# Layer 1 of a hybrid encoder: x brought into token form by VectorE block transposes and a trip through DRAM instead of TensorE transposes

## The chip, the cores and the metric

One Trainium2 chip, one of its cores. The metric is the device time of one execution in microseconds (us); lower is better. The kernel before was run three times: 1388.98, 1391.51 and 1394.25 us, median 1391.51 us. One more execution was profiled; it took 1389.59 us, and its span in the trace is 1387.7 us.

The engines are called by the names of the profile: PE (TensorE, matrix multiplication), PEld (its weight loads), DVE (VectorE), ACT (ScalarE), POOL (GpSimd) and SP (SyncE, which here only issues DMAs). Each engine works through its own list of instructions strictly in order; an instruction that waits holds up all that is behind it on its engine.

## What is computed

Two layers over 272 tokens (16 meta tokens and 256 frames) of width 2048, fp32 throughout. Layer 0 mixes gated linear attention and stick-breaking attention. Layer 1, the one that is changed, is a Mamba-2 mixer with 8 groups of 8 heads (head dimension 64, state 128). Cut to what matters here:

```python
z, xbc, dt_raw = split(h @ w_in)                 # 4096, 4096 + 2*1024, 64 columns
xbc = silu(causal_depthwise_conv(xbc))           # 4 taps
xs, bs, cs = split(xbc)                          # x: 8 groups x 8 heads x 64
dt  = softplus(dt_raw + dt_bias)
xdt = xs * dt[..., None]
a_cum = cumsum(dt * -exp(a_log))                 # per head
y = sum over s <= t of exp(a_cum[t] - a_cum[s]) * (c[t] . b[s]) * xdt[s]  + d_skip * xs
y = rms_norm_groups(y * silu(z), norm_w)
f = y @ w_out
h = layer_norm(ALPHA * h + f)
```

The kernel does not chunk: for one group it forms the matrix M (tokens s by tokens t, one for each head) = exp(decay difference) times (b . c), and y = xdt^T M. For that product xdt must lie with tokens on the partitions, while the projection, the convolution and the SiLU leave x with channels on the partitions. Bringing x from channel form into token form is what the change is about.

## The kernel before

**Weights and projections.** All large matmuls are done in three fp32r passes (high by high, high by low, low by high; helper `three`, lines L178 to L180, and L494 to L496 for the output projection). Weights come in units of 128 x 2048 fp32 (1 MB), loaded by SP on one queue (`load_unit`, L144) into three buffers `raw`, then cut in halves of 128 x 1024 into a high part `whi` (ACT, L159) and a low part `wlo` (DVE, a few on POOL, L160). There are five buffers for `whi` and `wlo` each. A unit that projects in (`in1`) is 48 matmuls of 256 to 272 columns, one that projects out (`out1`) 24 of 512 columns.

**Order of layer 1.** For each group g the units are B, C, x0, x1, x2, x3, z0, z1, z2, z3 (group 0: z0 before x0); from group 2 on, each group's ten units are followed by the four units of out1(g-2). While PE runs these units, side tasks advance by one step at each `tick` (four ticks in a unit); a bare `yield` in a task costs one tick. The instructions that come out of this are then ordered by a scheduler in the framework, engine by engine; a few runs of PE instructions are pinned together.

**The decays.** `dt_path` computes dt and the cumulated decays with heads on partitions, writes them to DRAM (`edr`), and takes their token form by small TensorE transposes into `est` and `est2` (the last 16 tokens). For each group `load_decay` (called by `post_B`, for group 0 by `decay1`) reads them back, broadcast over the partitions, into `ebc` (128 x 3328 fp32, 1664 KB, L1072). `ebc` lies in the buffer tagged `hacc`, of which there is one. `decay1` waits for the mixer of the group before, then makes M from `ebc` and `est` (L1105, L1106 on DVE, exp on ACT at L1108, the 16-token corner `mt` at L1112), and multiplies it by b . c (L1133). There is one buffer for M.

**The path of x.** Units x0 to x3 give four tiles of 128 channels x 272 tokens in `xt`. `post_x` does the convolution (L1050), and for each pair starts `x_path(g, j)`: SiLU (L1057, three ACT passes, the product at L1061), and for the second pair, after waiting steps, 8 TensorE transposes of 128 x 128 (L1173) and 4 of 128 x 16 (L1177) against the identity, into PSUM. DVE then multiplies by dt out of PSUM, into `xd` (four instructions, L1186) and `xd2` (four, the last 16 tokens, L1192).

**The mixer.** `mix_ssd` waits for the decay, x and z, then PE forms y = xdt^T M (L1235 with `xd` and M, L1241 with `xd2` and `mt2`), pinned in one block; DVE, POOL and ACT finish y (L1245 to L1255), PE sums the squares (L1261).

Of the kernel before, what the change touches and what calls it, by code (L numbers as in the profile page):

```python
# [6 lines left out]
F32 = mybir.dt.float32  # L7
F32R = mybir.dt.float32r
AF = mybir.ActivationFunctionType
ALU = mybir.AluOpType  # L10
PSUM = bass.MemoryType.PSUM

P = 128
D = 2048
KT = 16
NM = 16
S = 256
C0 = 12
NFIRST = 6
T = NM + S  # L20
# [10 lines left out]
NG, HPG = 8, 8  # L31
# [51 lines left out]
def _wait(*tasks):  # L83
    for t in tasks:
        while not t.done:
            yield


class _Body:
# [904 lines left out]
    def dt_path(self, ps, scr):  # L994
# [3 lines left out]
        H = 64  # L998
# [32 lines left out]
        self.est2 = lp.tile([16, 2, H], F32, tag="est2", name="est2")  # L1031
# [7 lines left out]
        vec.tensor_copy(self.est2.rearrange("p a h -> p (a h)"), pt[:16, 256:384])  # L1039
# [29 lines left out]
    def load_decay(self, g):  # L1069
        eb = self.hp.tile([P, HPG, 416], F32, tag="hacc", name=self.nm("ebc"))  # L1070
        src = self.edr[g * HPG : (g + 1) * HPG, :].rearrange("h c -> (h c)").partition_broadcast(P)
        self.nc.sync.dma_start(eb.rearrange("p h c -> p (h c)"), src)  # L1072
        self.cur["ebc", g] = eb
# [5 lines left out]
    def decay1(self, g):  # L1079
# [5 lines left out]
        if g:  # L1085
            yield from _wait(*self.mixers[6 + g - 1])
        else:
            yield from _wait(self.tasks["dt"], self.tasks["res"])
            self.load_decay(0)
            yield  # L1090
            yield
# [19 lines left out]
        e2 = self.est2[:, 0, g * HPG : (g + 1) * HPG].rearrange("p (h o) -> p h o", o=1).broadcast_to([16, HPG, 16])  # L1111
# [40 lines left out]
    def x_path(self, g, j):  # L1152
        nc, vec = self.nc, self.nc.vector
        xt = self.cur["x", g]
        xd = self.cur["xd", g]
        self.silu1(xt[:, j : j + 2, :].rearrange("p a t -> p (a t)"), vec)
        yield
        yield
        yield
        if g == 0:  # L1160
            yield from _wait(self.tasks["dt"])
        if j == 0:
            return
        for _ in range(5):
            yield
        pin = self.tc.keep_in_program_order

        pts = [self.po(), self.po()]
        p2 = self.zbank()
        for pt, jj in zip(pts, (0, 2)):  # L1170
            for i in range(2):
                for t in range(2):
                    pin(nc.tensor.transpose(  # L1173
                        pt[:, t * 256 + i * P : t * 256 + (i + 1) * P], xt[:, jj + i, t * P : (t + 1) * P], self.ident
                    ))
        for i in range(4):
            pin(nc.tensor.transpose(p2[:16, i * P : (i + 1) * P], xt[:, i, 256:T], self.ident))  # L1177
        yield
        hv = lambda a: a.rearrange("p (h c) -> p h c", c=64)
        bd = lambda a: a.rearrange("p (h o) -> p h o", o=1)  # L1180
        for pt, jj in zip(pts, (0, 2)):
            h0 = g * HPG + 2 * jj
            c = slice(jj * P, jj * P + 256)
            for t in range(2):
                d = bd(self.est[:, 1, t, h0 : h0 + 4]).broadcast_to([P, 4, 64])
                vec.tensor_tensor(hv(xd[:, t, c]), hv(pt[:, t * 256 : (t + 1) * 256]), d, op=ALU.mult)  # L1186
            yield
        e2 = bd(self.est2[:, 1, g * HPG : (g + 1) * HPG])
        for j in range(2):
            for p in range(2):  # L1190
                h = 4 * p + 2 * j
                vec.tensor_tensor(  # L1192
                    self.xd2[32 * j : 32 * j + 16, 2 * p : 2 * p + 2, :], hv(p2[:16, :])[:, h : h + 2, :],
                    e2[:, h : h + 2, :].broadcast_to([16, 2, 64]), op=ALU.mult,
                )
        yield
# [262 lines left out]
```

## Time and profile before

| what | value |
|---|---|
| runs, median (lowest to highest) | 1391.51 us (1388.98 to 1394.25) |
| profiled execution, its own time | 1389.59 us |
| span of the profiled execution | 1387.7 us |
| PE busy / DVE busy / ACT busy / POOL busy | 99% / 73% / 56% / 19% of the span |
| granted clock of PE | 1.00 of full speed |
| DMA | 249.83 MB, queue q1 takes 51.0% of the 16 DMA engines' span |
| layer 1 in the trace | from about 737 us to the end |

In the rows below, "busy" is time in which an engine executes; matmuls overlap, so the duration of one (0.28 us) is longer than the distance between the starts of two. "idle before <- releaser" is time in which the engine stood, and whose work ended it. Where a row counts a line's instructions, "x64" is how many there are.

### The profile page before, as it was taken

The numbers are of one execution on the slowest core, as the hardware profiler recorded it, in microseconds if no ns is written. First come the engines' busy times: TensorE is split into PE (matmuls) and PEld (weight loads), VectorE is DVE, ScalarE is ACT, GpSimd is POOL, SyncE is SP. The second block draws the span as 40 slices with busy tenths as digits, with TensorE's granted clock in tenths as the row PEclk, the third lists the DMA queues.
The fourth block names the chain that finished last, engine by engine and source line by source line (L and its number), as shares of the span: only waits on it lengthen the run. The fifth ranks groups of instructions, "written<-read, shape, count | busy, mean of one in ns | idle before, by whom it ended". The sixth has DMA issues, their size and how long they took to land.

```text
span 1387.7 us, 26097 instructions
## 1 busy us (share of the span) xinstructions
PE 1379.2 (99%) x10715; PEld 1328.3 (96%) x10715; DVE 1017.3 (73%) x1690; ACT 771.7 (56%) x1149; POOL 260.6 (19%) x253
## 2 busy tenths in 40 slices
PE   9999999999999999999999999999999999999998
PEld 8999999999999999999999999899898999989986
DVE  7857575574565565557899999787877778867687
ACT  6645454454345544556587677565565655656551
POOL 0000010100101000113500153331322323133221
PEclk9999999999999999999999999999999999999999
DMA  8544544445454445544354655465555556455561
GB/s 320 185 161 156 181 154 171 163 156 179 156 179 156 153 152 179 174 151 148 122 199 169 251 202 201 158 256 174 213 180 187 197 187 228 164 200 185 179 216 61
DMA packets 38007, 249.83 MB, mean 180 GB/s; under 512 B 4288, under 2 KB 6144, under 8 KB 9472
## 3 DMA queue, kind: packets, MB, share of 16 engines
q1 hardware_dynamic: 37168, 247.38, 51.0%
q8 instruction: 84, 1.38, 0.4%
q10 hardware_dynamic: 720, 0.79, 0.2%
q14 instruction: 35, 0.29, 0.1%
HBM read 245.94 MB, written 2.20 MB: 179 GB/s over the span
## 4 chain that ended last, share of the span: by engine, by line
PE 94%; DVE 3%; DMA 1%; ACT 1%; POOL 1%; issue 0%; SPq 0%; ACTq 0%; POOLq 0%; DVEq 0%
PE pj L179 25%; PE pj L178 25%; PE pj L180 25%; PE pj L494 4%; PE pj L496 4%; PE pj L495 4%; PE po L1235 1%; PE po L608 1%; DVE wlo L160 1%; PE po L1173 0%; DMA raw<-in_wts 0%; PE po L587 0%; PE z L1123 0%; POOL yu L1246 0%; DVE M L1105 0%
## 5 line engine op out<-in xcount | busy, mean ns | idle before, releaser
L178 PE MATMUL pj<-xhi,whi 128*128 128x272 f32 (+4 forms) x2560 | 732.1, 286 | 1.3 <-DVE fix L936 0.5
L179 PE MATMUL pj<-xlo,whi 128*128 128x272 f32 (+4 forms) x2560 | 730.8, 286 | 0.0
L180 PE MATMUL pj<-xhi,wlo 128*128 128x272 f32 (+4 forms) x2560 | 730.1, 286 | 0.0
L159 ACT ACTIVATE whi<-raw 128x1024 fp32r<-128x1024 f32 (+2 forms) x434 | 449.6, 1039 | 423.8 <-PE pj L179 350.7
L160 DVE TENSOR_TENSOR wlo<-raw,whi 128x1024 fp32r<-128x1024 f32 (+2 forms) x405 | 503.3, 1247 | 242.0 <-ACT whi L159 237.4
L178 PEld LDWEIGHTS pj<-xhi,whi 128*128 128x128 f32 x2560 | 482.1, 189 | 3.7 <-ACT whi L159 0.9
L179 PEld LDWEIGHTS pj<-xlo,whi 128*128 128x128 f32 x2560 | 482.1, 188 | 1.5 <-DVE wlo L160 0.4
L180 PEld LDWEIGHTS pj<-xhi,wlo 128*128 128x128 f32 x2560 | 481.9, 188 | 1.0 <-issue 0.8
L178 PE MATMUL pj<-mixh,whi 128*128 128x272 f32 x384 | 110.5, 289 | 0.0
L180 PE MATMUL pj<-mixh,wlo 128*128 128x272 f32 x384 | 110.5, 288 | 0.0
L179 PE MATMUL pj<-mixl,whi 128*128 128x272 f32 x384 | 110.4, 288 | 0.0
L160 POOL TENSOR_TENSOR wlo<-raw,whi 128x1024 fp32r<-128x1024 f32 x29 | 73.0, 2517 | 192.6 <-ACT whi L159 192.6
L494 PE MATMUL pj<-whi,yh 128*128 128x512 f32 (+1 forms) x240 | 93.3, 389 | 0.0
L495 PE MATMUL pj<-wlo,yh 128*128 128x512 f32 (+1 forms) x240 | 92.6, 386 | 0.0
L496 PE MATMUL pj<-whi,yl 128*128 128x512 f32 (+1 forms) x240 | 92.2, 386 | 0.0
L261 POOL TENSOR_TENSOR gr<-gr,gsc 128x1088 f32<-128x1088 f32 x6 | 15.4, 2568 | 308.2 <-ACT gsc L260 308.2
L179 PEld LDWEIGHTS pj<-mixl,whi 128*128 128x128 f32 x384 | 72.3, 188 | 0.2
L180 PEld LDWEIGHTS pj<-mixh,wlo 128*128 128x128 f32 x384 | 72.3, 188 | 0.1
L178 PEld LDWEIGHTS pj<-mixh,whi 128*128 128x128 f32 x384 | 72.2, 188 | 0.1
L503 DVE SCALAR_TENSOR_TENSOR acc<-pj,rr,acc 128x512 f32<-128x512 f32 (+1 forms) x65 | 46.5, 734 | 13.9 <-PE pj L496 13.9
L496 PEld LDWEIGHTS pj<-whi,yl 128*128 128x128 f32 x240 | 45.1, 188 | 9.1
L494 PEld LDWEIGHTS pj<-whi,yh 128*128 128x128 f32 x240 | 45.1, 188 | 9.0
(351 smaller groups left out, 1472.2 us busy)
## 6 DMA issues: line engine op xcount, KB each, us to landing
raw<-in_wts SPq DMA_DIRECT2D x212, 1024.0 KB, 4.8
ebc<-edr SPq DMA_DIRECT2D x8, 1664.0 KB, 6.7
raw<-in_wts SPq DMA_DIRECT2D x9, 256.0 KB, 6.4
hacc<-in_xT SPq DMA_DIRECT2D x7, 272.0 KB, 5.3
early<-in_wts SPq DMA_DIRECT2D x2, 512.0 KB, 6.5
lg<-in_lnr SPq DMA_DIRECT2D x1, 1024.0 KB, 4.7
lb<-in_lnr SPq DMA_DIRECT2D x1, 1024.0 KB, 5.3
out_h<-acc SPq DMA_DIRECT2D x2, 384.0 KB, 2.4
```

Of the source, the lines that this page charges most:

```text
L159: self.nc.scalar.activation(hi, src, AF.Copy)
L160: eng.tensor_tensor(lo, src, hi.bitcast(F32), op=ALU.subtract)
L178: mm(ps, whi, xhi, start=first, stop=False)
L179: mm(ps, whi, xlo, start=False, stop=False)
L180: mm(ps, wlo, xhi, start=False, stop=last)
L261: mul(c, c, e, op=ALU.mult)
L494: mm(ps, yh[:, kk, tt], hi[:, k, :], start=kk == 0, stop=False)
L495: mm(ps, yh[:, kk, tt], lo[:, k, :], start=False, stop=False)
L496: mm(ps, yl[:, kk, tt], hi[:, k, :], start=False, stop=kk == 3)
L503: self.nc.vector.scalar_tensor_tensor(a, ps, r[:, t : t + 1], a, op0=ALU.mult, op1=ALU.add)
L608: mm = lambda r, a, b, start=False, stop=False: self.nc.tensor.matmul(o[:, r], a, b, start=start, stop=stop, skip_group_check=True)
L1235: pin(mm(ov[p][i * 64 : (i + 1) * 64, jj, t0:S], xd[:, s, h * 64 : (h + 1) * 64], M[:, h, c0:c1], start=(s, jj) == (0, 0), stop=False, **gk,))
```

## The change

`x_path` no longer uses TensorE. Of the `hacc` buffer, whose 4352 columns `ebc` fills to 3328, the remaining 1024 columns become `xs`. After the SiLU of each pair DVE transposes the pair's 256 frame columns in blocks of 32 x 32 into `xs`, and the last 32 token columns into a new small tile `x9`. For the second pair SP then writes `xs` (512 KB) and `x9` (64 KB) to DRAM tiles `xdr` and `xdr9`; three ticks later it reads them back so that tokens come to lie on partitions: four DMAs of 128 KB into the place of `xs` (runs of 128 elements) and two of 16 KB into `xd2` (runs of 32). Three ticks later DVE multiplies by dt, now from SBUF: four instructions into `xd`, two in place in `xd2`. `est2` is kept on 48 partitions, with a second copy, for this. Since `xs` and `ebc` share one buffer, the next group's `load_decay` can only be issued when the products of this group have read `xs`. In `decay1`, groups after the first take three more ticks after the wait for the mixer before. The waits of `x_path` go from 3 and 5 ticks to 1, 3 and 3.

```diff
--- before.py
+++ after.py
@@ -1028,7 +1028,7 @@
         nc.sync.dma_start(self.edr, E[:, 16:432])
         yield
         self.est = lp.tile([P, 2, 2, H], F32, tag="est", name="est")
-        self.est2 = lp.tile([16, 2, H], F32, tag="est2", name="est2")
+        self.est2 = lp.tile([48, 2, H], F32, tag="est2", name="est2")
         yield from _wait(self.tasks["res"])
         pt = self.po()
         for n, a in enumerate((E[:, 0:128], E[:, 272:400], m[:, 0:128], m[:, 128:256])):
@@ -1036,7 +1036,8 @@
         for n, a in enumerate((E[:, 416:432], m[:, 256:272])):
             nc.tensor.transpose(pt[:16, 256 + n * H : 256 + (n + 1) * H], a, self.ident[:H, :H])
         vec.tensor_copy(self.est.rearrange("p a b h -> p (a b h)"), pt[:, :256])
-        vec.tensor_copy(self.est2.rearrange("p a h -> p (a h)"), pt[:16, 256:384])
+        for q in (0, 32):
+            vec.tensor_copy(self.est2[q : q + 16].rearrange("p a h -> p (a h)"), pt[:16, 256:384])
         yield
 
     def conv(self, src, ct, v, t0=0, lo=0):
@@ -1067,7 +1068,9 @@
             self.load_decay(g)
 
     def load_decay(self, g):
-        eb = self.hp.tile([P, HPG, 416], F32, tag="hacc", name=self.nm("ebc"))
+        eb = self.hp.tile([P, KT * T], F32, tag="hacc", name=self.nm("ebc"))
+        self.cur["xs", g] = eb[:, HPG * 416 :].rearrange("p (b c x) -> p b c x", c=4, x=32)
+        eb = eb[:, : HPG * 416].rearrange("p (h c) -> p h c", h=HPG)
         src = self.edr[g * HPG : (g + 1) * HPG, :].rearrange("h c -> (h c)").partition_broadcast(P)
         self.nc.sync.dma_start(eb.rearrange("p h c -> p (h c)"), src)
         self.cur["ebc", g] = eb
@@ -1084,6 +1087,9 @@
         yield
         if g:
             yield from _wait(*self.mixers[6 + g - 1])
+            yield
+            yield
+            yield
         else:
             yield from _wait(self.tasks["dt"], self.tasks["res"])
             self.load_decay(0)
@@ -1108,7 +1114,7 @@
                 act(M[:, h - 1 : h + 1, :], M[:, h - 1 : h + 1, :], AF.Exp)
                 yield
         mt = self.mt
-        e2 = self.est2[:, 0, g * HPG : (g + 1) * HPG].rearrange("p (h o) -> p h o", o=1).broadcast_to([16, HPG, 16])
+        e2 = self.est2[:16, 0, g * HPG : (g + 1) * HPG].rearrange("p (h o) -> p h o", o=1).broadcast_to([16, HPG, 16])
         vec.tensor_tensor(mt, eb[:16, :, 400:416], e2, op=ALU.subtract)
         vec.tensor_scalar(mt, mt, 0.0, None, op0=ALU.min)
         act(mt, mt, AF.Exp)
@@ -1155,44 +1161,51 @@
         xd = self.cur["xd", g]
         self.silu1(xt[:, j : j + 2, :].rearrange("p a t -> p (a t)"), vec)
         yield
-        yield
-        yield
-        if g == 0:
-            yield from _wait(self.tasks["dt"])
+        while ("ebc", g) not in self.cur:
+            yield
+
+        xs = self.cur["xs", g]
+        lp = self.lp
+        if j == 0:
+            self.cur["x9", g] = lp.tile([P, 4, 32], F32, tag="x9", name=self.nm("x9"))
+        x9 = self.cur["x9", g]
+        vec.transpose(xs[:, :, j : j + 2, :].rearrange("p b c x -> p c b x"), xt[:, j : j + 2, :S].rearrange("p c (b x) -> p c b x", x=32))
+        vec.transpose(x9[:, j : j + 2, :], xt[:, j : j + 2, 240:T])
         if j == 0:
             return
-        for _ in range(5):
-            yield
-        pin = self.tc.keep_in_program_order
-
-        pts = [self.po(), self.po()]
-        p2 = self.zbank()
-        for pt, jj in zip(pts, (0, 2)):
+
+        d = self.tc.dram_tile([4, 32, 8, P], F32, name=self.nm("xdr"))
+        d9 = self.tc.dram_tile([4, 32, 4, 32], F32, name=self.nm("xdr9"))
+        nc.sync.dma_start(d.rearrange("p t b x -> (p t) (b x)"), xs.rearrange("q b c x -> q (b c x)"))
+        nc.sync.dma_start(d9.rearrange("p t c x -> (p t) (c x)"), x9.rearrange("q c x -> q (c x)"))
+        for _ in range(3):
+            yield
+        xb = xs.rearrange("q b c x -> q (b c x)").rearrange("q (s p x) -> q s p x", s=2, p=4)
+        for b in range(4):
+            nc.sync.dma_start(
+                xb[32 * b : 32 * b + 32], d[:, :, b::4].rearrange("p t s x -> t s p x")
+            )
+        for i in range(2):
+            nc.sync.dma_start(
+                self.xd2[32 * i : 32 * i + 16].rearrange("t (n a) (b x) -> t n (a b) x", n=2, b=2),
+                d9[:, 16:, i::2].rearrange("p t n x -> t n p x"),
+            )
+        for _ in range(3):
+            yield
+
+        for t in range(2):
             for i in range(2):
-                for t in range(2):
-                    pin(nc.tensor.transpose(
-                        pt[:, t * 256 + i * P : t * 256 + (i + 1) * P], xt[:, jj + i, t * P : (t + 1) * P], self.ident
-                    ))
-        for i in range(4):
-            pin(nc.tensor.transpose(p2[:16, i * P : (i + 1) * P], xt[:, i, 256:T], self.ident))
-        yield
-        hv = lambda a: a.rearrange("p (h c) -> p h c", c=64)
-        bd = lambda a: a.rearrange("p (h o) -> p h o", o=1)
-        for pt, jj in zip(pts, (0, 2)):
-            h0 = g * HPG + 2 * jj
-            c = slice(jj * P, jj * P + 256)
-            for t in range(2):
-                d = bd(self.est[:, 1, t, h0 : h0 + 4]).broadcast_to([P, 4, 64])
-                vec.tensor_tensor(hv(xd[:, t, c]), hv(pt[:, t * 256 : (t + 1) * 256]), d, op=ALU.mult)
-            yield
-        e2 = bd(self.est2[:, 1, g * HPG : (g + 1) * HPG])
-        for j in range(2):
-            for p in range(2):
-                h = 4 * p + 2 * j
-                vec.tensor_tensor(
-                    self.xd2[32 * j : 32 * j + 16, 2 * p : 2 * p + 2, :], hv(p2[:16, :])[:, h : h + 2, :],
-                    e2[:, h : h + 2, :].broadcast_to([16, 2, 64]), op=ALU.mult,
-                )
+                o = xd[:, t, :].rearrange("q (c i a x) -> q c i a x", c=4, i=2, a=2)[:, :, i]
+                x = xb[:, t, 2 * i : 2 * i + 2].rearrange("q a (c x) -> q c a x", c=4)
+                e = self.est[:, 1, t, g * HPG + i : (g + 1) * HPG : 2].rearrange("q (c o u) -> q c o u", o=1, u=1)
+                vec.tensor_tensor(o, x, e.broadcast_to([P, 4, 2, 32]), op=ALU.mult)
+            yield
+        for i in range(2):
+            q = slice(32 * i, 32 * i + 16)
+            x = self.xd2[q].rearrange("t (n h) c -> t n h c", n=2)
+            e = self.est2[q, 1, g * HPG : (g + 1) * HPG].rearrange("t (n j h) -> t j n h", n=2, j=2)[:, i]
+            e = e.rearrange("t n (h u) -> t n h u", u=1)
+            vec.tensor_tensor(x, x, e.broadcast_to([16, 2, 2, 64]), op=ALU.mult)
         yield
 
     def post_z(self, ps, g, j):
```

How the instructions move. On SP, the loads around the last decays and around the x of group 6 (groups counted from 0; `ebc_14656` before and `ebc_14650` after are the decays of group 7). Before, that load stands among the weight loads of out1(4):

```order
L144 DMA raw_13552<-in_wts 128x2048
L144 DMA raw_13598<-in_wts 128x2048
L1072 DMA ebc_14656<-edr 128x3328
L144 DMA raw_13648<-in_wts 128x2048
L144 DMA raw_13714<-in_wts 128x2048
```

After, SP issues it behind the round trip of group 6, whose weight units are those of z and of out1(4) of that group:

```order
L144 DMA raw_14361<-in_wts 128x2048
L1179 DMA xdr_14129<-ebc_13707 128x1024
L1180 DMA xdr_1732_14130<-x_1716_13970 128x128
L144 DMA raw_14408<-in_wts 128x2048
L1185 DMA ebc_13707<-xdr_14129 32x8x128 x4
L1189 DMA xd_8126<-xdr_1732_14130 16x8x32 x2
L144 DMA raw_14490<-in_wts 128x2048
L1075 DMA ebc_14650<-edr 128x3328
L144 DMA raw_14536<-in_wts 128x2048
```

The load of the next decays has moved from one group ahead to some 12 weight loads later, behind two writes and six reads of which the reads wait for the writes.

On DVE, group 6 from the product of the SiLU to the first instructions of the next M. Before:

```order
L1061 TENSOR_TENSOR xt_13861<-xt_13861,xcl_14111 128x544
L160 TENSOR_TENSOR wlo_14273<-raw_14159,whi_14272 128x1024
L160 TENSOR_TENSOR wlo_14311<-raw_14219,whi_14310 128x1024
L1057 TENSOR_SCALAR xcl_14252<-gz_14157 128x512
L1186 TENSOR_TENSOR xd_13862<-po_14238,est 128x256 x2
L1186 TENSOR_TENSOR xd_13862<-po_14239,est 128x256 x2
L1192 TENSOR_TENSOR xd_8126<-z_64,est_8718 16x128 x4
L160 TENSOR_TENSOR wlo_14339<-raw_14219,whi_14338 128x1024
```

After (L1172 and L1173 are the transposes, L1201 and L1208 the products):

```order
L1062 TENSOR_TENSOR xt_13837<-xt_13837,xcl_14105 128x544
L1172 STREAM_TRANSPOSE ebc_13707<-xt_13837 128x2x8x32
L1173 STREAM_TRANSPOSE x_1716_13970<-xt_13837 128x64
L160 TENSOR_TENSOR wlo_14305<-raw_14231,whi_14304 128x1024
L1058 TENSOR_SCALAR xcl_14252<-gz_14157 128x512
L160 TENSOR_TENSOR wlo_14333<-raw_14231,whi_14332 128x1024
L160 TENSOR_TENSOR wlo_14366<-raw_14301,whi_14365 128x1024
L1201 TENSOR_TENSOR xd_13838<-ebc_13707,est 128x4x64 x4
L1208 TENSOR_TENSOR xd_8126<-xd_8126,est_8718 16x256 x2
L160 TENSOR_TENSOR wlo_14413<-raw_14361,whi_14412 128x1024
```

The products stand one split of a weight half later than before, behind the DMAs that bring x back; the transposes come in front of them.

On PE, the mixer of group 1 (`xd_9242`). Before it stands inside the second unit (C) of group 2:

```order
L180 MATMUL pj_9876<-xhi,wlo_9803 128x260
L1235 MATMUL po_9893<-M_9452,xd_9242 64x256 x4
L1235 MATMUL po_9894<-M_9452,xd_9242 64x256 x4
L1235 MATMUL po_9893<-M_9452,xd_9242 64x144 x4
L1235 MATMUL po_9894<-M_9452,xd_9242 64x144 x4
L1241 MATMUL po_9893<-mt_8125,xd_8126 64x2x16 x2
```

After it stands where unit x1 of group 2 ends and x2 (`pj_10136`) begins:

```order
L180 MATMUL pj_10061<-xhi,wlo_10026 128x272
L1248 MATMUL po_9892<-M_9506,xd_9242 64x256
L178 MATMUL pj_10136<-xhi,whi_10062 128x272
L1248 MATMUL po_9892<-M_9506,xd_9242 64x256 x3
L1248 MATMUL po_9893<-M_9506,xd_9242 64x256 x4
```

It has moved 133 projection matmuls later; group 0's by 76 or less. From group 2 on the mixers stand at the same place among the projections (within 3 matmuls in group 2, exactly from group 3 on).

## Rows read from the trace of the kernel before

**Rows 1.** The page, busy time of each engine, share of the span, instructions

```profile
PE 1379.2 (99%) x10715; PEld 1328.3 (96%) x10715; DVE 1017.3 (73%) x1690; ACT 771.7 (56%) x1149; POOL 260.6 (19%) x253
```

**Rows 2.** The page, the chain that ended last, share of the span by engine

```profile
PE 94%; DVE 3%; DMA 1%; ACT 1%; POOL 1%; issue 0%; SPq 0%; ACTq 0%; POOLq 0%; DVEq 0%
```

**Rows 3.** Busy time by stretch: us, PE, PEld, DVE, ACT, POOL, clock, DMA, GB/s

```profile
764.00:790.00 26.00, 26.00 (x206) 24.02 (x207) 25.31 (x50) 17.87 (x25) 4.72 (x3) 1.00 0.69 256
...
1148.00:1233.00 85.00, 85.00 (x644) 80.05 (x643) 66.92 (x105) 50.15 (x70) 23.55 (x18) 1.00 0.54 194
```

**Rows 4.** Timeline of PE in group 7: start, duration, line, operation

```profile
1296.75 0.28 PE L180 MATMUL pj<-xhi,wlo 128*128 128x256 f32 x1
1296.87 0.60 PE L1173 MATMUL po<-ident,xt 128*128 128x128 f32 x4
...
1297.43 0.28 PE L179 MATMUL pj<-xlo,whi 128*128 128x256 f32 x1
...
1298.91 0.28 PE L180 MATMUL pj<-xhi,wlo 128*128 128x256 f32 x1
1299.03 0.60 PE L1173 MATMUL po<-ident,xt 128*128 128x128 f32 x4
1299.46 0.60 PE L1177 MATMUL z<-ident,xt 128*16 128x128 f32 x4
...
1300.02 0.28 PE L179 MATMUL pj<-xlo,whi 128*128 128x256 f32 x1
```

**Rows 5.** By tile or line: count, duration in ns (least/median/most), first and last start

```profile
L1173 PE MATMUL po<-ident,xt x64: 270/273/329, 763.7 to 1299.4; 128*128 128x128 f32 x64
L1177 PE MATMUL z<-ident,xt x32: 272/273/273, 771.1 to 1299.8; 128*16 128x128 f32 x32
L1061 DVE TENSOR_TENSOR xt<-xt,xcl x16: 704/725/1423, 753.4 to 1296.0; 128x544 f32<-128x544 f32 x16
...
L1186 DVE TENSOR_TENSOR xd<-po,est x32: 403/414/425, 765.1 to 1300.0; 128x256 f32<-128x256 f32 x32
...
L1192 DVE TENSOR_TENSOR xd<-z,est x32: 269/270/283, 772.1 to 1302.2; 16x128 f32<-16x128 f32 x32
...
L1072 SPq DMA_DIRECT2D ebc<-edr x8: 326/327/331, 763.7 to 1155.9; - x8
```

**Rows 6.** DMA issues: count, KB each, median us to landing

```profile
raw<-in_wts SPq DMA_DIRECT2D x212, 1024.0 KB, 4.8
ebc<-edr SPq DMA_DIRECT2D x8, 1664.0 KB, 6.7
...
out_h<-acc SPq DMA_DIRECT2D x2, 384.0 KB, 2.4
...
raw<-in_wts SPq DMA_DIRECT2D x3, 128.0 KB, 3.6
```

**Rows 7.** Timeline, group 6: end of x's SiLU, mixer, next M, next split

```profile
1209.59 0.72 DVE L1061 TENSOR_TENSOR xt<-xt,xcl 128x544 f32<-128x544 f32 x1 [0.37 <-ACT xcl L1060]
...
1229.67 2.93 PE L1235 MATMUL po<-M,xd 128*64 128x256 f32 x32
...
1232.65 0.35 DVE L1105 TENSOR_SCALAR M<-ebc,est 128x256 f32<-128x256 f32 x1 [1.50 <-PE po L1235]
...
1238.62 1.21 DVE L160 TENSOR_TENSOR wlo<-raw,whi 128x1024 fp32r<-128x1024 f32 x1
...
1243.90 0.39 PE L494 MATMUL pj<-whi,yh 128*128 128x512 f32 x1
```

**Rows 8.** Timeline, group 2: end of x's SiLU, and the mixer

```profile
874.66 0.72 DVE L1061 TENSOR_TENSOR xt<-xt,xcl 128x544 f32<-128x544 f32 x1 [0.58 <-ACT xcl L1060]
...
889.19 2.93 PE L1235 MATMUL po<-M,xd 128*64 128x256 f32 x32
```

**Rows 9.** Waits in layer 1: who waited for whom, us in total, times, longest

```profile
ACT whi L159 <- PE pj L179: 97.6, 77, 4.7
...
ACT whi L159 <- DMA raw<-in_wts: 4.4, 3, 1.8
```

**Rows 10.** Waits of SP's queue in layer 1, same columns

```profile
SPq L1072 <- DVE M L1106: 52.5, 5, 12.5
```

## The prediction

> **What bounds the kernel now.** I read the page's busy times first: PE is busy for 99% of the span and DVE for 73% [rows 1]. The chain that ended last is PE for 94% and DVE for 3% [rows 2]. That is an average, so I then looked at stretches of layer 1: from 1148 to 1233 us, which holds group 6, PE is busy 85.00 of 85 us and DVE 66.92; from 764 to 790 us, where the x of groups 0 and 1 lies, PE is busy 26.00 of 26 but DVE 25.31 [rows 3]. Last the waits: the high parts of the weights wait for PE to give back a buffer 77 times, 97.6 us in all, and for a weight load 3 times, 4.4 us [rows 9]. So weights stand ready before PE wants them, and each us of PE work taken out of layer 1 is a us gained unless something else becomes late.
>
> **What goes from PE.** A projection matmul begins 0.12 us after the one before it; more closely, 13 begin from 1297.43 to 1298.91, 0.114 each [rows 4]. Between the L180 at 1296.75 and the L179 at 1297.43 stand four transposes and one L178: 0.68 less two distances, 0.45 us for four. Between 1298.91 and 1300.02 stand eight and one L178: 1.11 − 0.23 = 0.88. A group's twelve cost 1.34 us. There are 64 + 32 of them [rows 5], eight groups, so 8 × 1.34 = 10.7 us goes. That is the whole gain to be had, 0.8%.
>
> The Trainium skill ("VectorE: DVE Perf Modes", section "The three transpose paths") has 390 ns for a TensorE transpose of 128 x 128 in bf16; by it 96 × 0.39 = 37 us would go and the run come to about 1354. The trace disagrees: the next transpose does not wait for the one before, and a distance of 0.11 us decides.
>
> **What comes to DVE.** Per group two transposes of 512 elements a partition, two of 64, four products L1201 of 256 elements and two L1208. No row shows a block transpose. Its bounds: 0.41 us (L1186, 256 elements [rows 5]) and 1.21 (the split L160, 1024 elements [rows 7]); I take 0.72, the product L1061 with 544 elements [rows 5]. The small ones go at the 0.27 of L1192, L1201 and L1208 at the 0.41 of L1186. New: 2 × 0.72 + 2 × 0.27 + 6 × 0.41 = 4.4. Gone: 4 × 0.41 + 4 × 0.27 = 2.7. Net +1.7 us a group, from +1.1 to +2.7 by the bounds. In groups 2 to 7 the 18 us in 85 in which DVE stands [rows 3] hide it. In groups 0 and 1 DVE has 0.7 us free in 26, and what comes to it there can make a split late: between 0 and 2 × 1.7 = 3.4; I take 1.5. The second copy into `est2` is one small instruction, hidden before layer 1's groups begin.
>
> **The round trip.** Count from T0, the end of the second pair's SiLU product. Transposes 0.72 + 0.27 = 1.0. Then the write of 512 KB: between the 2.4 us of `out_h` (384 KB, into DRAM) and the 4.8 of a weight load (1024 KB) [rows 6]; nearest by size and kind is `out_h`, so 3. Then six reads issued in a row, each holding SP for 0.33 (L1072 [rows 5]); the four big ones are out after 1.3, and the last lands 3.6 after its issue as the 128 KB loads do [rows 6]: 4.9. With a weight load in front on the queue, 4.8 more. Products 4 × 0.41 = 1.6; a split in front of them and L1208 behind, 1.2 + 0.8 = 2.0. Sum T0 + 12.5; without the split, with 2.4 for the write and one read's 3.6, 8.6 or a little less; with the slow write and a weight load in front of the reads, T0 + 19.1.
>
> What is allowed: in group 6 T0 is 1209.59 + 0.72 = 1210.31 and the mixer begins at 1229.67, 19.4 later [rows 7]; without the transposes' 1.3, 18.0. Groups 3 to 7 keep their mixers at the same place among the projections, and group 6 stands for them. So 12.5 fits with 5.5 to spare, and 19.1 is late by 1.1. Group 2 is tighter: 889.19 − 875.38 = 13.8 [rows 8], less 1.3 = 12.5; the cost there lies between 0 and 19.1 − 12.5 = 6.6, and I take 1. The mixers of groups 0 and 1 have moved later by up to 76 and 133 matmuls (up to 8.6 and 15 us at 0.114), which makes room for the trip.
>
> The same page and section of the Trainium skill warn that a plain DMA whose access pattern transposes is 19 times slower than the transposing one where the innermost stride of the destination is large. The reads here keep runs of 512 and 128 bytes on both sides, so I weigh it only in rival B; no row shows such a read.
>
> **The next decays and SP.** L1075 now waits for the products, at about T0 + 10.5 (without the split and L1208) to 13, where L1072 had been a group ahead. Queued behind it on SP are the weight loads. It lands 6.7 later [rows 6], 11.5 with a weight load in front: T0 + 17 to 24.5. M begins at 1232.65, right behind the mixer [rows 7], T0 + 22.3, less 1.3: 21.0. So M may be up to 3.5 late. On DVE the next split of a weight stands behind M: it ends at 1238.62 + 1.21 = 1239.83, and PE uses its unit's first half at 1243.90 [rows 7]. These 4.1 us cover it; I take 0. If that cover were gone it would be 3.5 × 6 = 21. As for weights, SP stood up to 12.5 us at L1072 before, waiting for M [rows 10], and PE stayed busy; now it stands in three shorter pieces (write behind the transposes, reads behind the write, decays behind the products), together about 12, with a weight load let through between each. I take 0 here too.
>
> **Sum.** 10.7 − 1.5 − 1 = 8.2. The profiled execution, 1389.59, would come to 1381.4. It lies 1.9 under the median of the runs, 1391.51, so on that the forecast is 1383.3.
>
> **Rivals.**
>
> A. The gain is eaten. DVE is full in groups 0 and 1 and two DMA trips in a row stand before M. For it: 25.31 of 26 [rows 3], and only 4.1 us of cover behind M [rows 7]. Against: the chain has DVE at 3%. Price: 3.4 for groups 0 and 1, 4 for group 2, 0.3 in each of five groups for M: 8.9, so 1391.5 − 10.7 + 8.9 = 1389.7; with parts of it, 1385.5 to 1391.5.
>
> B. Slower. The reads land late and PE stands before L1248, with everything behind it, in groups 2 to 7. It decides at T0 + 18.0; what breaks even is 10.7 lost over six groups with group 2 losing 5.5 more than the others: 5.2 / 6 = 0.9, at T0 + 18.9; slower by 0.5% (7 us, about what a measurement of this kernel can tell from no change) from T0 + 20.0. At T0 + 21.5 it costs 5 × 3.5 + 9 = 26.5, hence 1391.5 − 10.7 + 26.5 = 1407. For it: the upper bound 19.1, strided reads that no row shows, a queue busy with weights. Against: to be slower by 0.5% the write and the reads would have to take 15.4 us, nearly twice the 7.9 that I take.
>
> C. The transposes weren't binding: PE stands as long as they took, since DVE or ACT deliver halves no faster. For it: DVE's 25.31 of 26. Against: 77 waits of ACT on PE and 3 on loads [rows 9]. It gives 1391.5.
>
> **Numbers.** Forecast 0.58, its own range 1380.5 to 1386. A 0.25, B 0.12, C 0.05. The forecast's case is faster by over 0.5% (under 1384.5) with 0.85 of its chance, 0.49; A adds little, 0.02: faster 0.51. Same: the rest of it, A's and C's, and 0.02 of B: 0.09 + 0.23 + 0.05 + 0.02, rounded to 0.38. Slower 0.11. The range runs from 1380, a little below 1391.5 − 10.7, to 1392, which leaves out most of B and a small rest on both sides.
>
> **What would show it.** Right: no transposes of x on PE in layer 1's groups; in the window of group 6 PE busy throughout, with its group 1.3 us shorter; L1201 waiting on DVE for a read that ends by T0 + 13; the block transposes at 0.4 to 1.2 us. Wrong: idle time of PE before L1248 with `xd` as the releaser (B); M's first instruction waiting for `ebc`, and PE waiting for a split behind it, or the stretch from 760 to 790 longer than before (A); PE less busy with its groups as long as before (C). A block transpose of 512 elements much over 1.2 us would break the DVE term and put the gain of the first groups in doubt.

## The result and the profile after

Seven runs of the changed kernel took 1393.85 to 1397.98 us, median 1396.03; the kernel before, beside them, 1389.36. The recorded ratio is 1.0042, interval 1.0032 to 1.0052 (the quotient of the two medians is 1.0048): slower by some 6 us, where 8 us less were forecast, and above the range. The profiled execution has a span of 1394.3 us against 1387.7.

The page of the changed kernel, busy times and the chain, as [rows 1, 2]:

```profile
PE 1374.4 (99%) x10619; PEld 1323.7 (95%) x10619; DVE 1032.7 (74%) x1707; ACT 772.0 (55%) x1149; POOL 257.9 (18%) x253
...
PE 87%; DVE 7%; DMA 4%; issue 1%; SPq 1%; ACT 0%; POOL 0%; ACTq 0%; DVEq 0%
```

PE has lost 4.8 us of busy time where 10.7 were taken from its work, and the span less PE's busy time has grown from 8.5 to 19.9 us. The shares of DVE and DMA in the chain have grown, from 3% and 1% to 7% and 4%. Who made PE wait in the groups of layer 1 (engine, line, who was waited for: us, times, longest); before, no such wait was over 0.5 us (one of 1.2 us for ACT at the end of the layer stands in both):

```profile
PE pj L494 <- DVE acc L503: 5.2, 2, 2.9
PE pj L178 <- ACT gz L1215: 4.4, 1, 4.4
PE z L1129 <- DVE bcp L1101: 1.9, 1, 1.9
```

The third, at 869.9 us in front of group 2's product b . c, was not followed up.

Stretches of the changed kernel, with the columns of [rows 3]:

```profile
764.00:790.00 26.00, 26.00 (x212) 25.54 (x212) 24.60 (x46) 18.82 (x27) 3.91 (x3) 1.00 0.81 261
819.00:840.00 21.00, 20.67 (x147) 20.67 (x148) 16.96 (x24) 14.36 (x25) 5.25 (x4) 0.85 0.69 216
1148.00:1233.00 85.00, 84.90 (x635) 79.50 (x635) 67.51 (x106) 50.72 (x72) 24.70 (x18) 1.00 0.65 221
```

The second of them before:

```profile
819.00:840.00 21.00, 21.00 (x187) 19.96 (x186) 20.88 (x44) 14.88 (x24) 9.70 (x7) 1.00 0.54 189
```

After the 4.4 us wait, which ends at 819.3, the granted clock is 0.85 for these 21 us: part of them at the lower of the two levels (1.2 instead of 2.4 GHz). PE is "busy" for 20.67 of them and gets through 147 matmuls instead of 187. 0.15 × 21 = 3.2 us, which no wait shows; over the whole run the mean clock of 0.996 is worth some 5 to 6 us, an estimate (0.004 × 1394). So the 11.4 us of new waiting came with about half as much again.

Comparing when the same projection matmul starts in both traces tells where this lies. Some records of matmuls are missing, so the match is good to half a us. From 767 to 916 us, groups 0 to 2, the changed kernel falls back by some 9.5 us although it has 4.0 us less PE work: about 13.5 lost. In group 4 it falls back by 3.2 more, which is 4.5 with its own saving of 1.34. Groups 3, 5, 6 and 7 gain 1 to 1.7 each, about as forecast.

**The wait near 818 us.** Group 0 in the kernel before: the mixer's first matmul starts at 783.82, and the four instructions that finish y on DVE are these (start, duration):

```profile
796.67 0.85 DVE L1245 SCALAR_TENSOR_TENSOR yu<-xt,cpk,po 128x256 f32<-128x256 f32 x2
...
803.22 0.47 DVE L1245 SCALAR_TENSOR_TENSOR yu<-xt,cpk,po 128x256 f32<-128x256 f32 x1
...
804.01 0.47 DVE L1245 SCALAR_TENSOR_TENSOR yu<-xt,cpk,po 128x256 f32<-128x256 f32 x1
```

After (L1258 is the same instruction, L1139 the products of group 1's M, L249 a causal select, L1215 moves z out of PSUM):

```profile
791.16 0.65 PE L1248 MATMUL po<-M,xd 128*64 128x256 f32 x2
...
798.13 0.87 DVE L1258 SCALAR_TENSOR_TENSOR yu<-xt,cpk,po 128x256 f32<-128x256 f32 x2
...
808.24 0.46 DVE L1258 SCALAR_TENSOR_TENSOR yu<-xt,cpk,po 128x256 f32<-128x256 f32 x1
...
809.45 6.45 POOL L249 TENSOR_SCALAR_AFFINE_SELECT cb<-cb 16x16 f32<-16x16 f32 x1
809.49 0.46 DVE L1258 SCALAR_TENSOR_TENSOR yu<-xt,cpk,po 128x256 f32<-128x256 f32 x1
...
811.02 3.68 DVE L1139 TENSOR_TENSOR M<-M,cb 128x800 f32<-128x800 f32 x4
...
815.77 0.69 DVE L1172 STREAM_TRANSPOSE ebc<-xt 128x512 f32<-128x512 f32 x1
815.87 1.40 POOL L1259 TENSOR_TENSOR yu<-yu,gz 128x256 f32<-128x256 f32 x2
816.62 0.51 ACT L1261 ACTIVATE yh<-yu,cpk 128x256 fp32r<-128x256 f32 x1 [6.70 <-POOL yu L1259]
...
818.92 0.91 ACT L1215 ACTIVATE gz<-pj 128x256 f32<-128x256 f32 x3
819.33 0.59 PE L178 MATMUL pj<-xhi,whi 128*128 128x272 f32 x1 [4.45 <-ACT gz L1215]
```

Read it from the end. PE wants a PSUM buffer that ACT has not emptied; ACT stands 6.7 us in front of L1261, which waits for POOL; POOL is held by a tiny select; and y's second half left DVE 5 us later than before. Group 0's mixer, whose result y is, came 7.3 us later; that this alone makes y late is not shown (in nodma, below, the mixer comes 3.6 us later than before and y 14).

**The waits for L503.** Group 2 after the change, from the product of x's SiLU on:

```profile
884.80 0.71 DVE L1062 TENSOR_TENSOR xt<-xt,xcl 128x544 f32<-128x544 f32 x1
...
886.29 0.33 SPq L1179 DMA_DIRECT2D xdr<-ebc  x1
...
888.96 2.53 SPq L1185 DMA_DIRECT2D ebc<-xdr  x4
...
895.20 1.66 DVE L1201 TENSOR_TENSOR xd<-ebc,est 128x256 f32<-128x256 f32 x4 [4.23 <-DMA ebc<-xdr]
...
896.89 0.33 SPq L1075 DMA_DIRECT2D ebc<-edr  x1
...
903.53 2.29 DVE L1111 TENSOR_SCALAR M<-ebc,est 128x256 f32<-128x256 f32 x1 [1.40 <-DMA ebc<-edr]
...
909.98 1.39 DVE L503 SCALAR_TENSOR_TENSOR acc<-pj,rr,acc 128x512 f32<-128x512 f32 x2
...
910.86 0.47 PE L494 MATMUL pj<-whi,yh 128*128 128x512 f32 x1 [2.26 <-DVE acc L503]
```

The trip ends 896.86 − 885.51 = 11.4 us after T0. Only then the next decays are asked for, they land 6.6 later, M is late, and L503, which empties the output projection's PSUM, stands behind M on DVE. Group 4 shows the same (2.9 us).

### The profile page after: what moved, and what is told of

Its sections match the earlier page's. It is cut to its first block, busy times and chain, and to the rows that moved or that the text cites. A ratio compares the mean times of both kernels' runs of the same rounds, so it can differ in the third digit from the quotient of the medians.

```text
span 1394.3 us, 25997 instructions
## 1 busy us (share of the span) xinstructions
PE 1374.4 (99%) x10619; PEld 1323.7 (95%) x10619; DVE 1032.7 (74%) x1707; ACT 772.0 (55%) x1149; POOL 257.9 (18%) x253
## 4 chain that ended last, share of the span: by engine, by line
PE 87%; DVE 7%; DMA 4%; issue 1%; SPq 1%; ACT 0%; POOL 0%; ACTq 0%; DVEq 0%
PE pj L179 24%; PE pj L178 24%; PE pj L180 24%; PE pj L494 3%; PE pj L496 3%; PE pj L495 3%; DMA ebc<-edr 1%; PE po L608 1%; DVE wlo L160 1%; DMA xdr<-ebc 1%; DMA ebc<-xdr 1%; PE po L1248 1%; DVE M L1111 1%; DVE M L1139 1%; DVE M L1112 1%
## 5 line engine op out<-in xcount | busy, mean ns | idle before, releaser
L178 PE MATMUL pj<-xhi,whi 128*128 128x272 f32 (+4 forms) x2560 | 732.3, 287 | 5.4 <-ACT gz L1215 4.4
L160 DVE TENSOR_TENSOR wlo<-raw,whi 128x1024 fp32r<-128x1024 f32 (+2 forms) x405 | 504.7, 1251 | 235.3 <-ACT whi L159 234.6
L178 PEld LDWEIGHTS pj<-xhi,whi 128*128 128x128 f32 x2560 | 483.4, 189 | 8.2 <-ACT gz L1215 4.7
L178 PE MATMUL pj<-mixh,whi 128*128 128x272 f32 x384 | 110.5, 289 | 0.0
L160 POOL TENSOR_TENSOR wlo<-raw,whi 128x1024 fp32r<-128x1024 f32 x29 | 75.0, 2586 | 151.6 <-ACT whi L159 151.6
L178 PEld LDWEIGHTS pj<-mixh,whi 128*128 128x128 f32 x384 | 72.2, 188 | 0.1
L495 PEld LDWEIGHTS pj<-wlo,yh 128*128 128x128 f32 x240 | 45.5, 190 | 8.8
```

Source lines behind the costliest of these rows:

```text
L160: eng.tensor_tensor(lo, src, hi.bitcast(F32), op=ALU.subtract)
L178: mm(ps, whi, xhi, start=first, stop=False)
L495: mm(ps, yh[:, kk, tt], lo[:, k, :], start=False, stop=False)
```

## Experiments

Five rounds each. "before" is 1388.9 to 1389.4 us beside every one. Differences in the text are of medians unless a ratio is named; runs of one kernel spread by up to 7 us (own: 1389.5 to 1396.2).

| kernel | median us | ratio to before (95%) |
|---|---|---|
| the changed kernel | 1396.03 | 1.0042 (1.0032 to 1.0052) |
| nopet | 1381.89 | 0.9947 (0.9935 to 0.9959) |
| nopet_e | 1388.59 | 0.9995 (0.9986 to 1.0003) |
| nopet_l | 1381.44 | 0.9945 (0.9932 to 0.9959) |
| own | 1393.32 | 1.0032 (1.0023 to 1.0042) |
| small | 1395.88 | 1.0049 (1.0037 to 1.0061) |
| own_small | 1391.67 | 1.0022 (1.0013 to 1.0030) |
| nodma | 1389.68 | 1.0000 (0.9992 to 1.0009) |
| dvex | 1389.91 | 1.0006 (0.9997 to 1.0014) |
| nopet_e_dvex | 1387.31 | 0.9986 (0.9977 to 0.9994) |
| nomul | 1391.11 | 1.0017 (1.0008 to 1.0026) |
| ybefore | 1390.74 | 1.0011 (1.0003 to 1.0020) |
| noy | 1394.93 | 1.0051 (1.0038 to 1.0065) |
| own_noy | 1395.05 | 1.0037 (1.0023 to 1.0050) |
| hyb1 | 1385.90 | 0.9975 (0.9966 to 0.9985) |
| hyb2 | 1383.53 | 0.9957 (0.9945 to 0.9970) |
| hyb3 | 1382.91 | 0.9958 (0.9945 to 0.9970) |
| hyb3n | 1383.47 | 0.9955 (0.9942 to 0.9969) |
| hyb3a | 1385.86 | 0.9975 (0.9965 to 0.9985) |

**What the TensorE transposes were worth.** nopet takes them out of the kernel before:

```diff
-        pts = [self.po(), self.po()]
-        p2 = self.zbank()
...
-                vec.tensor_tensor(hv(xd[:, t, c]), hv(pt[:, t * 256 : (t + 1) * 256]), d, op=ALU.mult)
+                vec.tensor_tensor(hv(xd[:, t, c]), hv(xt[:, jj + t, :256]), d, op=ALU.mult)
```

> The kernel before, with the twelve TensorE transposes of x of each group left out; the products with dt read untransposed x from SBUF, the same number and size of VectorE instructions (so the output is not the reference's). If PE bounds and the transposes cost what their rows say, 10.7 us go: about 1379, ratio 0.992. If the transposes were not binding (PE would stand for them anyway), 1388 to 1390, ratio 0.999 to 1.000. Between them: the products now have two inputs in SBUF and may disturb GpSimd, which would show as idle time of PE behind ACT or POOL.

nopet_e does so for `g <= 2` alone, nopet_l for `g >= 3`.

> The kernel before with the TensorE transposes left out in groups 0 to 2 alone, the products there reading untransposed x from SBUF (so the output is not the reference's): 4.0 us of PE work less. Theory 3 (PE is not what sets the pace there): nothing gained or worse, 1389 to 1393, ratio 1.000 to 1.003, with a wait of PE and a lower clock near 815 to 840 us. Rival (PE work is gained everywhere, the loss of the changed kernel comes from the trip and VectorE): 1385 to 1386, ratio 0.997.

> The same in groups 3 to 7 alone: 6.7 us of PE work less. Theory 3: all of it is gained, 1382 to 1383.5, ratio 0.995 to 0.996. Rival (only part of it is): 1385 or more.

In groups 3 to 7 all is gained: 0.55% of 1389 is 7.6 us (5.7 to 9.4 by the interval), 6.7 were worked out. In groups 0 to 2 the 4.0 us less work bring 0.7, and the interval includes no change. PE waits 1.9 us for POOL and 0.3 for ACT there instead. PE was all but 100% busy in that stretch before, and yet over half of the work taken from it turned into waiting for other engines. DVE was as full (28.79 of 29 us from 790 to 819).

How much of this the experiment made itself is open. Its products L1189 read x from SBUF, where the kernel before reads PSUM, and two of them stand in the run of DVE instructions beside which POOL's product took 6.26 us instead of 0.7:

```profile
805.72 0.41 DVE L1189 TENSOR_TENSOR xd<-xt,est 128x256 f32<-128x256 f32 x1
805.94 6.26 POOL L1249 TENSOR_TENSOR yu<-yu,gz 128x256 f32<-128x256 f32 x1 [0.64 <-DVE yu L1248]
806.05 3.68 DVE L1133 TENSOR_TENSOR M<-M,cb 128x800 f32<-128x800 f32 x4
809.66 0.41 DVE L1189 TENSOR_TENSOR xd<-xt,est 128x256 f32<-128x256 f32 x1
...
818.42 0.62 PE L1264 MATMUL po<-ones,ysq 128*128 128x16 f32 x4 [1.93 <-POOL ysq L1258]
```

The expectation of nopet had named this; no run separates it.

nopet has the same two waits; the stretch behind them, in nopet and then in nopet_e:

```profile
819.00:840.00 21.00, 21.00 (x159) 19.67 (x160) 17.91 (x40) 14.44 (x26) 5.64 (x5) 0.85 0.45 154
```

```profile
819.00:840.00 21.00, 21.00 (x183) 19.67 (x183) 21.00 (x44) 17.23 (x30) 8.20 (x7) 1.00 0.57 198
```

The clock fell in one and not in the other, so what such a wait costs is not fixed. It differs between executions of one kernel too: nopet's five runs took 1379.5 and 1379.6 us at a clock of 1.000, 1381.9 to 1383.7 at 0.997 or 0.998. nopet_e's six at 0.999 or 1.000 took 1387.6 to 1388.6, its five at 0.997 or 0.998 1389.2 to 1390.6.

**Late decays.** own makes the buffer one lasting tile, so that the load waits only for what it overwrites:

```diff
-        eb = self.hp.tile([P, KT * T], F32, tag="hacc", name=self.nm("ebc"))
+        if g == 0:
+            self.ebt = self.hp.tile([P, KT * T], F32, tag="hacc", name="ebt")
+        eb = self.ebt
```

> The changed kernel, but the buffer of the decays is one lasting tile, so that the load of the next decays waits only for the readers of the last decays and not for the products that read xs; it goes out a group ahead again, as before the change. Theory 1 (the stalls of PE at 910 and 1081 us, 2.3 and 2.9 us, and the lower clock behind them come from decays that are loaded behind the round trip): those two stalls go, 1388 to 1391, ratio to before 0.999 to 1.001. Rival (the stalls come from VectorE's added work): the stalls stay, ratio 1.003 to 1.005.

The waits for L503 fall from 5.2 to 0.3 us, but the time by 2.7 only, where 5 to 8 were expected; by the ratios it is 1.4, and the two intervals overlap. The wait near 818 is 4.6 ("PE pj L178 <- ACT gz L1217: 4.6, 1, 4.6"). A new wait of 1.4 us for M at an output projection has come.

**GpSimd held by VectorE.** small moves one line:

```diff
+        self.causal(cb[:16, 0:16], 16, False)
         self.causal(cb[:, 16:128], 112, False, 16)
         self.causal(cb[:, 272:400], 128, False)
-        self.causal(cb[:16, 0:16], 16, False)
```

> The changed kernel, with the three causal selects of GpSimd in another order (the 16x16 one first). Theory 2 (at 809 to 816 us GpSimd's 16x16 select takes 6.45 us instead of 0.19 because VectorE works without a gap through six instructions with two inputs in SBUF; ScalarE stands behind GpSimd and holds a PSUM bank, PE waits 4.4 us and then runs at a lower clock): with the select done before that stretch the 4.4 us and the lower clock go, 1388 to 1390, ratio 0.999 to 1.000. Rival (VectorE is simply full there and PE would wait anyway): PE's wait at 815 to 820 us stays within 1 us, ratio 1.003 to 1.005.

> Both edits together. If theories 1 and 2 both hold and add up: 1396 less about 7 less about 7, 1381 to 1384, ratio 0.994 to 0.996. If VectorE's added work is behind both: 1393 to 1396, ratio 1.003 to 1.005. One of the two alone: about 1389, ratio 0.999 to 1.000.

The theory of the select falls, the holding stays. The select is done early, and the next instruction of POOL is held for as long (POOL, then PE, in small):

```profile
810.91 6.32 POOL L1259 TENSOR_TENSOR yu<-yu,gz 128x256 f32<-128x256 f32 x1 [0.62 <-DVE yu L1258]
```

```profile
817.70 0.59 PE L178 MATMUL pj<-xhi,whi 128*128 128x272 f32 x1 [2.76 <-ACT gz L1215]
```

PE's wait is 2.8 instead of 4.4, the clock behind it 0.88, the time the same. In own POOL is hardly held (its products of y there take 0.75 and 1.57 us, and it waits 5.5 us for y from DVE), and PE still waits 4.6: y is late either way. own_small differs from own by less than the intervals.

**The trip.** nodma leaves out L1179 to L1189; the products read the block transposes as they stand.

> The changed kernel without the trip through DRAM: no writes and reads of x, the products read the block transposes as they stand (so the output is not the reference's); transposes, products, waits and the load of the decays behind the products stay. Theory 1 (late decays because of the trip) gives back the stalls at 910 and 1081 us: 1387 to 1391, ratio 0.999 to 1.002, with the wait near 815 us left, as VectorE is as full as before. Rival (the trip is also what spoils groups 0 to 2): that wait goes too, 1380 to 1384, ratio 0.994 to 0.996.

6.3 us come back, but PE's wait near 818 is 5.4 us, at a clock of 0.85. So the DMAs of x are not what makes that wait. That is 3.6 us more than own gave back; what the trip costs beside the late decays was not traced.

**VectorE's added work.** dvex adds to the kernel before:

```diff
+        if g < 2:
+            x9 = self.lp.tile([P, 2, 32], F32, tag="x9", name=self.nm("x9"))
+            for _ in range(4):
+                vec.transpose(x9, xt[:, j : j + 2, 240:T])
```

> The kernel before with added VectorE work alone: in groups 0 and 1 four block transposes of 128 x 64 for each pair into an unused tile, 1.6 us a group, nothing else. Theory 3: PE gets a wait at 790 to 825 us, and 3 to 8 us come on top, 1392 to 1397, ratio 1.002 to 1.006. Rival (VectorE has room there, the stall of the changed kernel comes from the later place of the mixers or the DMAs): 1389 to 1390, ratio 1.000 to 1.001.

> The kernel without the transposes in groups 0 to 2 and with 1.6 us of added VectorE work in each of groups 0 and 1 (so the output is not the reference's). If the two add up: 1.3 us more than without the added work. If they compound (a later VectorE meets an earlier PE): 3 to 6 us more, 1393 to 1398.

Theory 3 is that in groups 0 to 2 VectorE and what hangs on it set the pace. Neither result is what it said. The added work costs 0 to 2 us, and together with less PE work the kernel is a little faster than with that alone. In nopet_e_dvex PE waits 0.9 us for a split on DVE and not for POOL, and the clock is 0.999 or 1.000 in all eleven runs. nomul takes VectorE work away, in own and in group 1 alone:

```diff
-        for h in range(0, HPG, 2):
+        for h in range(0, HPG if g != 1 else 0, 2):
             c = cb[:, 16:416].rearrange("p (o c) -> p o c", o=1).broadcast_to([P, 2, 400])
```

> The kernel with the lasting tile of the decays, with the four products of M with b . c (3.7 us of VectorE at 811 to 816 us) left out in group 1 alone (so the output is not the reference's). Theory 3 (VectorE sets the pace between 790 and 822 us): PE's wait of 4.6 us there falls under 1.5 us and the lower clock behind it goes, 1386 to 1389 against 1393 with the products. Rival (ScalarE or the order of the mixer sets it): the wait stays over 3 us and the time at 1392 to 1394.

The wait at 818 falls from 4.6 to 0.7 ("PE pj L178 <- ACT gz L1217: 0.7, 1, 0.7") and the clock from 819 to 840 stays at 1.00, so DVE is on that chain. But 2.2 us are gained, not 4 to 7: waits of up to 2.3 us for POOL's `ysq` and for L503 come up behind it.

**The yields.** ybefore adds the three yields to the kernel before, noy takes them from the changed kernel, own_noy from own.

> The kernel before with the three extra yields ahead of M alone. If M's later place costs by itself: a wait of PE at 815 to 825 us or at the first matmul of an output projection, 1391 to 1396, ratio 1.002 to 1.005. If not: 1389 to 1390, ratio 1.000 to 1.001.

> The changed kernel without the three extra yields ahead of M. If the yields are part of the loss in groups 0 to 2 (M of group 1 comes 6.4 us later than before): the wait near 818 us shrinks and 1390 to 1394. If they cost nothing or help: 1395 to 1400.

> All groups on the new path, the lasting tile, no extra yields ahead of M. If M of group 1 standing 6 us later in VectorE's order, ahead of the end of y of group 0, makes the wait near 818 us: that wait falls under 2 us and 1385 to 1389, ratio 0.997 to 1.000. If the later mixer of group 0 makes it without that: the wait stays over 3 us, 1391 to 1394.

They cost the kernel before 0 to 3 us. Without them the changed kernel's wait at 818 shrinks to 1.8 us, but PE then waits for L503 four times, 6.3 us, and for `xd` 3.2: no gain. In own_noy the wait at 818 grows to 6.6, so with the lasting tile the yields do not make it. M of group 1 starts at nearly the same time with and without them: there is one buffer for M, and group 0's mixer, which is late, reads it until 795 to 798 us. What goes with PE's wait is the last instruction of group 0's y on DVE (times in us, read from the traces):

| kernel | mixer of group 0 starts | M of group 1 starts | last y of group 0 starts | PE's wait there |
|---|---|---|---|---|
| before | 783.8 | 793.3 | 804.0 | 0 |
| hyb1 (below) | 783.7 | 792.6 | 804.6 | 0 |
| nomul | 793.8 | 800.6 | 812.9 | 0.7 |
| noy | 791.6 | 800.1 | 812.7 | 1.8 |
| after | 791.2 | 799.7 | 809.5, held on POOL to 815.9 | 4.4 |
| own | 794.1 | 800.8 | 817.0 | 4.6 |
| nodma | 787.5 | 798.7 | 818.0 | 5.4 |
| own_noy | 793.6 | 800.3 | 817.9 | 6.6 |

The last row's two last instructions of y:

```profile
814.94 0.47 DVE L1257 SCALAR_TENSOR_TENSOR yu<-xt,cpk,po 128x256 f32<-128x256 f32 x1
...
817.89 0.47 DVE L1257 SCALAR_TENSOR_TENSOR yu<-xt,cpk,po 128x256 f32<-128x256 f32 x1
```

**Which groups.** hyb1, hyb2 and hyb3 are own with groups below K = 1, 2 and 3 on the old path (TensorE transposes, no yields, also none ahead of the M of group K); hyb3n is hyb3 without yields, hyb3a is hyb3 with the buffer as in the change:

```diff
         self.silu1(xt[:, j : j + 2, :].rearrange("p a t -> p (a t)"), vec)
+        if g < K:
+            yield from self.x_old(g, j)
+            return
```

> The lasting tile of the decays, group 0 on the old path, groups 1 to 7 on the new one. If the loss is group 0's (its mixer stands 98 matmuls later with the lasting tile, and with it M of group 1 and the end of y of group 0): 1382 to 1385, ratio 0.995 to 0.997, no wait at 815 us. If it is group 1's: 1387 to 1392, ratio 0.999 to 1.002.

> As the kernel with groups 0 to 2 on the old path, but group 2 on the new one too. If group 2 has room for the trip: 0.7 to 1.3 us less than that kernel, 1381.5 to 1382.5. If its shorter way from x to the mixer is too short: a wait of PE at 890 to 915 us and 1384 to 1387.

> Groups 0 to 2 as before the change (TensorE transposes, no extra yields), groups 3 to 7 by the new path, with the lasting tile of the decays. Theory 3 (in the stretch of groups 0 to 2 VectorE and what hangs on it set the pace, so PE work saved there is only turned into waiting, and each wait is paid a second time at a lower clock; the saving is real from group 3 on): the stalls at 815 and 910 us go, five groups gain 0.7 to 1.3 each, 1382.5 to 1386, ratio 0.995 to 0.998. Rival (the round trip costs as much in the later groups as it saves): 1388 to 1391, ratio 1.000.

> The same without the three extra yields before M in groups 4 to 7. With the decays loaded a group ahead they have nothing to wait for: the same as the kernel with them within 1.5 us, 1382 to 1386. Rival (the yields keep M out of the way of the mixer's products): 1 to 3 us longer than with them.

> Groups 0 to 2 on the old path, groups 3 to 7 by the change as it was made: the decays are loaded behind the products. Theory 1 (late decays cost about 4.4 us in group 4 and little in the others): 1386 to 1388, ratio 0.998 to 0.999, 3 to 5 us more than with the lasting tile, with a wait of PE for L503 at an output projection. Rival (no late decays once groups 0 to 2 run as before): 1382 to 1384.

With group 0 alone back, 7.4 us come back (1393.3 to 1385.9), and the wait near 818 is gone:

```profile
790.00:819.00 29.00, 29.00 (x258) 28.31 (x255) 28.91 (x61) 22.22 (x37) 9.36 (x11) 1.00 0.56 201
```

Group 1 costs 2.4 more (hyb1 against hyb2). Group 2 costs and gains nothing that can be told, where hyb2 was expected 0.7 to 1.3 under hyb3. The late decays, from hyb3a against hyb3, are worth 3.0 us (2.4 by the ratios); the waits for L503 in the two, hyb3a first:

```profile
PE pj L494 <- DVE acc L503: 2.6, 1, 2.6
```

```profile
PE pj L494 <- DVE acc L503: 1.0, 1, 1.0
```

hyb2, hyb3 and hyb3n beat both kernels, by 0.42 to 0.45% against before, and cannot be told apart.

## Why the prediction was wrong

- **The transposes' price: right, its place wrong.** 1.34 us a group agrees with what the later groups gained (7.6 us over five, 1.5 each), and the 0.39 us that the Trainium skill ("VectorE: DVE Perf Modes", section "The three transpose paths") gives for one did not show: nopet gained 7 us, not 37. The first step that failed is "8 × 1.34 = 10.7 us goes". It took PE's 26.00 of 26 [rows 3] and the halves that waited for PE [rows 9] for proof that PE sets the pace of groups 0 to 2. Three groups' saving is worth 0.7 us there, not 4.0 (nopet_e), part of which may be that experiment's own doing.
- **The mixers of groups 0 and 1: the step that turned the sign.** The text said that they "have moved later by up to 76 and 133 matmuls (up to 8.6 and 15 us at 0.114), which makes room for the trip", and asked nothing more. Behind group 0's mixer stand y on DVE, then POOL, ACT and a PSUM buffer of z for which PE waits. The new path of group 0 costs 7.4 us and that of group 1 2.4 (own, hyb1, hyb2), where 1.5 was taken for both. By ratios, groups 0 to 2 were forecast at −1.5 us and came to +10.2 (own against hyb3): 11.7 of the 14 us between the forecast and the result.
- **DVE's work.** Its size was right: 0.705 us for a large transpose, 0.2 for a small one, 0.42 for most products. The reason for charging it was not: such work alone costs 0 to 2 us (dvex). Taking 3.7 us of DVE work from that chain does clear most of the wait (nomul). That it is DVE's order there and not its sum that counts is an inference from these two.
- **The round trip.** 12.5 us forecast, 10.5 to 15.3 to the last product into `xd` in groups 2 to 7; PE hardly waited for it. Two sizes in it were too small: a read holds SP for 0.61 us, not 0.33, and the large ones land 5.6 us after their issue, not 3.6. In groups 0 and 1 the trip took 22.6 and 25.1, since write and reads landed 6 to 7 us after their issue, with weight loads on the same queue, and DVE had other work in front of the products. The 19-fold price of which the Trainium skill warns in the same section is against a transposing DMA, which no run here has. Against a plain load of 128 KB, 3.8 us, such a read took 5.6, with runs that stay whole on both sides.
- **The next decays: 0 was wrong, the reason with it.** In groups 2 and 4 M starts 7.5 and 8.3 us after the mixer's first matmul instead of 3.0 [rows 7], 4.5 and 5.3 late where up to 3.5 was forecast. The cover of 4.1 us was read from a split that stands behind M; PE waited for L503, which stands there too. It is worth 1.4 to 3.0 us in all (own; hyb3a against hyb3; by ratios and by medians).
- **The clock** stood in no term. It was worth some 5 to 6 us in the profiled execution.
- **The rivals.** A named the right two places and reached 1391.5; it lacked the clock and the chain behind group 0's mixer. For A the text charged DVE's sum. B did not happen, though the kernel is slower: PE waited 0.2 us in all for `xd`. C, at 0.05, came true in part for groups 0 to 2: the saved time turned into waiting (nopet_e).

By ratios to before the sum is now: nopet_l −7.6; the new path's own cost in groups 3 to 7 +1.8 (hyb3 −5.8); groups 1 and 2 +2.3 (hyb1 −3.5); group 0 +7.9 (own +4.4); late decays +1.4 (after +5.8). What stays open is what in the new path of group 0 makes its mixer and y late. PE comes to the mixer with at most 0.2 us of waiting, so the mixer stands later in PE's list of instructions; y stands later in the list of a DVE that is busy for 28.46 of 29 us. Why the scheduler orders them so was not looked into. Selects, yields, trip and added VectorE work were each changed alone; some shortened the wait, only the products left out in nomul nearly removed it, and no remedy other than the old path was found.

## What to carry to other kernels

An engine that is 100% busy need not be the only one that sets the pace; ask of each stretch what stands ready ahead of it, or take its work out of that stretch alone and time it, and check what else the edit changes. When an instruction block moves later, follow what is behind it on every engine down to the buffer that somebody else wants back, before calling the move "room". A shared buffer is a wait: after a change that couples two tiles, list what now loads late and all that queues behind its reader, not just the first.

## What the runs showed of the hardware

- A POOL instruction (a select, at least 0.19 us; a product, 0.7) stood 6.3 to 6.5 us while DVE ran L160, four L1139 and L160 without a gap, all with both inputs in SBUF, and went on when a one-input transpose came (after, small). The Trainium skill ("SBUF — State Buffer", section "Who interferes with whom") says that a DVE instruction with two SBUF inputs contends with a GpSimd instruction that reads SBUF. The trace agrees, and shows that a run of six can hold it to the end of the run.
- A wait of 1.9 us was followed by 21 us at a granted clock of 0.85 in one execution (nopet) and at 1.00 in another (nopet_e) with the same waits up to there.
- A DMA issue whose source is transposed by its access pattern (32x8x128) held SP for 0.61 us, a plain one for 0.33.
